# A hybrid decoder layer in three-product fp32: the mixer's values two heads at a time, and four smaller reorderings

## The chip, the cores and the metric

The kernel runs on one core of one Trainium2 chip. The metric is the time on the device in microseconds (us). Five engines work side by side, each through its own list of instructions: TensorE (PE; its weight loads are shown apart as PEld), VectorE (DVE), ScalarE (ACT), GpSimd (POOL) and SyncE (SP), which here issues most of the transfers.

## The reference

One layer of a decoder trunk for a prompt of 512 tokens and 8 samples of 8 tokens each (576 columns together, T; the prompt's 512 are TP, the samples' 64 are TS), model width 1024:

```python
# x -> x + post(Wout[concat(Mamba2-SSD heads, mLSTM heads)](pre(x)))   one combined input projection
# x -> x + post(CrossAttn(pre(x), memory K/V))
# x -> x + post(SwiGLU(pre(x)))                                        RMSNorm before and after each
SSM_HEADS, SSM_HEAD_DIM, SSM_GROUPS, SSM_STATE = 16, 64, 2, 128
ML_HEADS, ML_V_DIM, ML_QK_DIM = 4, 256, 128
N_MEM, X_HEADS, X_HEAD_DIM = 256, 4, 256
```

Three parts matter here. The SSD part computes for every head y = (C B^T * exp(segment sums, causal)) (dt x) plus the carried state's share. The mLSTM part has values v = u Wv of 4 heads x 256 columns. The cross attention of the prompt is softmax(q k^T) v over 256 memory rows, then a projection by the weights wxo.

## The kernel before, in words

Activations lie transposed in SBUF: 128 features by 576 columns, eight such blocks for the width. Every product of the projections is made of three matmuls: an operand is cast to a high part (`uh`, `whi`) and the rest is a low part (`ul`, `wlo`), and high x high, high x low and low x high are summed in PSUM. Weights come in units of 128 x 1024 (512 KB): `split_w` has SP load a unit into one of two buffers `raw`, ACT casts it to `whi` (L179), DVE takes the difference `wlo` (L186; in some tiles half of it is made by ACT and a transfer that adds). `whi` and `wlo` have three buffers each.

PSUM has eight banks of 512 columns: three in the pool `GP` (projections, values), three in `MP`, two in `BP`. A scheduler reorders the program by its own estimate of the times; `tc.issue_after(x)` makes what stands under it come later than x in that order, without a wait of its own. The order that it finds is fixed when the kernel is built; on the chip each engine takes its list in order and waits on semaphores.

The start (L295 to L346): `NWARM` dummy products warm PE up; the first two weight tiles come in quarters beside the blocks of x. Per block, ACT makes `uh` (L318) and DVE `ul` (L319); per quarter, a cast (L190) and a difference (L191). The products of these tiles are at L333 to L335. The fourth tile of the input weights, `w2`, is loaded whole into the buffer of the first (L336) and used at L200 to L203, the lines of the common `gemm`.

The values (`gemm_tok` with `v_evac`): for each of four heads two units of weights; the stationary operand is a block of tokens, the moving one the 256 columns of one head. Two token blocks share one bank. The 64 sample tokens use two narrower products instead of three. Each bank is copied out by ACT (L794), scaled by the norm.

The SSD part (`ssd_prompt`) runs over two groups and four pairs of heads. Per pair: `ps_l` (L615) spreads the segment sums, DVE adds the mask's terms (L618, four per head), ACT takes the exponential (L620), DVE multiplies by C B^T (L621), giving `lm`; then `ps_yi` (L626) is the product with x, `ps_ec` (L630) and `ps_yn` (L636) the carried state's share, which DVE multiplies (L638). The products of the values and, behind them, of the z projection (`ps_in`, L200 to L203) are put in between. What copies z out of its banks (L962 to L966) uses memory that the SSD part still holds, so those banks stay full until the last pair is done.

The attention: `ps_at` (scores, L1285 to L1287), their maximum and exponential `pr` (L1290 to L1294), `attn_values` with `ps_ov` (L1315 to L1317) and its split into `qh` and `ql` (L190, L191, into `oh`, `ol`). `ps_os` (L1342) are the samples' products with cached values, which come by transfers `kva` and `kvb`. `xo` (L1438) loads the weights wxo of the attention's output projection. `rstd_rows` (L243) spreads a norm's factors, one column per token block, over rows by transposes on PE (L251) and a copy.

## Time and profile before

| | |
|---|---|
| median of 3 runs | 1099.72 us (1099.5 to 1101.24) |
| the profiled execution | 1100.06 us |
| its span, first to last instruction | 1098.0 us |
| PE busy | 1087.5 us |
| PEld busy | 1041.8 us |
| DVE busy | 753.6 us |
| ACT busy | 610.3 us |
| POOL busy | 229.7 us |
| granted clock of PE | 0.998 |
| moved by the transfers | 181.25 MB |

The terms below are made against the profiled execution; 2.06 us of it lie outside its span. A row of a timeline has the start, the duration, the engine, the line, the operation with its tiles (output <- inputs), the shape, and how many alike follow each other (xN); in brackets, the idle time ahead of it on its engine and what ended it. Matmuls overlap, so the spacing of their starts, and not the duration, is what one costs. A row of waits has the sum, the number and the longest.

### The profile page before, as it was taken

The page shows a single profiled execution, that of the slowest core. Times are in us where ns is not written, and L with a number is a line of the kernel's source. Part 1 is how long each engine was busy: PE and PEld are TensorE (multiplying, and loading weights), DVE is VectorE, ACT ScalarE, POOL GpSimd, SP SyncE. Part 2 cuts the span into 40 slices and gives each one's busy share as a digit, 9 for nine tenths or more (in the row PEclk, how much of TensorE's full clock was granted, in tenths as well). Part 3 has the DMA queues.
Part 4 walks back from the last instruction along what each step waited for, and adds up shares of the span by engine and source line. Part 5 has one row for each costly group of instructions (what it writes and reads, how often), then busy time and mean ns, then how long its engine had stood idle before and what let it go on. Part 6 is the DMA issues. An engine that isn't in the chain of part 4 may idle for free.

```text
span 1098.0 us, 21177 instructions
## 1 busy us (share of the span) xinstructions
PE 1087.5 (99%) x8355; PEld 1041.8 (95%) x8355; DVE 753.6 (69%) x1507; ACT 610.3 (56%) x1105; POOL 229.7 (21%) x305
## 2 busy tenths in 40 slices
PE   9999999999999999999999999999999999999997
PEld 8999888998999999999988879999999999999997
DVE  6896776558877775659654456676557877788555
ACT  6877523346654565555544445645566566656654
POOL 1443544223213112000244301100011111111000
PEclk9999999999999999999999999999999999999999
DMA  6785544335745349553468764645386687578532
GB/s 211 186 148 128 154 144 155 125 88 154 203 137 162 102 146 310 183 194 102 153 206 282 252 223 156 227 165 114 93 199 139 144 199 180 120 181 191 130 130 87
DMA packets 58679, 181.25 MB, mean 165 GB/s; under 512 B 6572, under 2 KB 11820, under 8 KB 58068
## 3 DMA queue, kind: packets, MB, share of 16 engines
q1 hardware_dynamic: 42452, 136.85, 38.0%
q0 software_dynamic: 15552, 41.95, 19.4%
q8 instruction: 65, 1.06, 0.4%
q10 hardware_dynamic: 576, 1.11, 0.3%
q14 instruction: 34, 0.28, 0.1%
HBM read 159.23 MB, written 20.65 MB: 164 GB/s over the span
## 4 chain that ended last, share of the span: by engine, by line
PE 94%; DMA 3%; DVE 1%; ACT 1%; issue 0%; POOL 0%; SPq 0%; DVEq 0%; ACTq 0%; POOLq 0%
PE ps_in L200 7%; PE ps_in L201 7%; PE ps_in L203 7%; PE ps_o L201 3%; PE ps_o L203 3%; PE ps_o L200 3%; PE ps_g L1792 3%; PE ps_g L1793 3%; PE ps_g L1794 3%; PE ps_u L1792 3%; PE ps_u L1794 3%; PE ps_u L1793 3%; PE ps_dn L1792 2%; PE ps_dn L1793 2%; PE ps_dn L201 2%; PE ps_dn L200 2%
## 5 line engine op out<-in xcount | busy, mean ns | idle before, releaser
L200 PE MATMUL ps_in<-uh,whi 128*128 128x320 f32 (+1 forms) x544 | 163.6, 301 | 0.0
L203 PE MATMUL ps_in<-uh,wlo 128*128 128x320 f32 (+1 forms) x544 | 163.5, 301 | 0.0
L201 PE MATMUL ps_in<-ul,whi 128*128 128x320 f32 (+1 forms) x544 | 162.6, 299 | 0.0
L179 ACT CAST whi<-raw 128x1024 fp32r<-128x1024 f32 (+1 forms) x102 | 102.9, 1012 | 95.5 <-PE ps_in L201 28.6
L186 DVE TENSOR_TENSOR wlo<-raw,whi 128x512 fp32r<-128x512 f32 (+1 forms) x94 | 95.2, 1014 | 68.6 <-ACT whi L179 67.6
L200 PEld LDWEIGHTS ps_in<-uh,whi 128*128 128x128 f32 x544 | 103.1, 190 | 2.3 <-issue 1.7
L203 PEld LDWEIGHTS ps_in<-uh,wlo 128*128 128x128 f32 x544 | 103.1, 190 | 1.2 <-issue 0.4
L201 PEld LDWEIGHTS ps_in<-ul,whi 128*128 128x128 f32 x544 | 103.2, 190 | 0.6
L184 POOL DMA_DIRECT2D wlo<-win x32 | 27.7, 875 | 86.9 <-ACT wlo L183 78.8
L1792 PE MATMUL ps_g<-b,whi 128*128 128x288 f32 x144 | 42.5, 295 | 0.0
L1793 PE MATMUL ps_g<-b,whi 128*128 128x288 f32 x144 | 42.4, 295 | 0.0
L1793 PE MATMUL ps_u<-b,whi 128*128 128x288 f32 x144 | 42.4, 295 | 0.0
L1792 PE MATMUL ps_u<-b,whi 128*128 128x288 f32 x144 | 42.4, 295 | 0.0
L1765 ACT CAST whi<-rawx 128x1024 fp32r<-128x1024 f32 (+1 forms) x26 | 25.6, 986 | 27.8 <-PE ps_dn L1793 13.8
L191 DVE TENSOR_TENSOR wlo<-sw,whi 128x1024 fp32r<-128x1024 f32 (+1 forms) x26 | 29.6, 1139 | 14.9 <-ACT whi L190 14.8
L200 PE MATMUL ps_xo<-qh,whi 128*128 128x288 f32 x128 | 38.6, 303 | 0.2 <-ACT whi L179 0.2
L201 PE MATMUL ps_o<-mixs_l,whi 128*128 128x320 f32 (+1 forms) x128 | 38.2, 299 | 0.0
L203 PE MATMUL ps_o<-mixm_h,wlo 128*128 128x256 f32 (+1 forms) x128 | 38.2, 298 | 0.0
L201 PE MATMUL ps_xo<-ql,whi 128*128 128x288 f32 x128 | 37.9, 297 | 0.1
L201 PE MATMUL ps_xq<-u2l,whi 128*128 128x320 f32 (+1 forms) x128 | 38.0, 298 | 0.0
L201 PE MATMUL ps_o<-mixm_l,whi 128*128 128x256 f32 (+1 forms) x128 | 38.0, 296 | 0.0
L200 PE MATMUL ps_xq<-u2h,whi 128*128 128x320 f32 (+1 forms) x128 | 37.9, 300 | 0.0
(769 smaller groups left out, 3927.6 us busy)
## 6 DMA issues: line engine op xcount, KB each, us to landing
raw<-win SPq DMA_DIRECT2D x35, 512.0 KB, 3.7
raw<-wout SPq DMA_DIRECT2D x17, 512.0 KB, 3.6
raw<-wxq SPq DMA_DIRECT2D x13, 512.0 KB, 3.8
raw<-wgate SPq DMA_DIRECT2D x13, 512.0 KB, 4.4
raw<-wup SPq DMA_DIRECT2D x13, 512.0 KB, 5.1
wlo<-win POOLq DMA_DIRECT2D x24, 256.0 KB, 5.6
kva<-kc SPq DMA_DIRECT2D x12, 512.0 KB, 5.9
kva<-vc SPq DMA_DIRECT2D x12, 512.0 KB, 5.0
```

The lines of the kernel that those rows point to most:

```text
L179: A.copy(hi[:, :n], raw[:, :n])
L184: G.dma_start(lo[:, a:b], src[:, a:b], accum_op=ALU.add)
L186: e.tensor_tensor(lo[:, a:b], raw[:, a:b], hi[:, a:b].bitcast(F32), op=ALU.subtract)
L191: (eng or V).tensor_tensor(lo, src, hi.bitcast(F32), op=ALU.subtract)
L200: mm(ps, wh, ah, start=i == 0, stop=False)
L201: mm(ps, wh, al, start=False, stop=False)
L203: m = mm(ps, tiles[order[c]][1], xh(order[c], t0, n), start=False, stop=c == len(tiles) - 1)
L1765: A.copy(s.h3[:, s.all], s.r2[:, s.all])
L1792: mm(ps, wh, b[0][k], start=start and k == 0, stop=False, skip_group_check=True)
L1793: mm(ps, wh, b[1][k], start=False, stop=False, skip_group_check=True)
L1794: m = mm(ps, wl, b[0][k], start=False, stop=k == nk - 1, skip_group_check=True)
```

## The change

Five edits. (1) The start: 21 dummy products instead of 24; the first block of x is split in two halves; the quarters' casts and differences are put behind the copy of their block. (2) The values of two heads at once: the moving operand has 512 columns, one token block fills one bank; four units of weights per two heads; the first three token blocks go through units 0 to 3, then the last two through units 1, 2, 3 and 0, where unit 0 is loaded again. (3) Two calls of `rstd_rows` for the samples' norm spread only the samples' column. (4) `split` returns its cast. (5) The first three wxo weights are put behind the cast of the sixth attention output.

```diff
-NWARM = 24
+NWARM = 21
...
     def split(hi, lo, src, eng=None, cast=None):
-        (cast or A.copy)(hi, src)
+        c = (cast or A.copy)(hi, src)
         (eng or V).tensor_tensor(lo, src, hi.bitcast(F32), op=ALU.subtract)
+        return c
...
-        xd = (A if k < 2 else S).dma_start(xraw[:, k, :], I["xT"][:, k, :])
-        if k == 1:
+        xd = (S if k else A).dma_start(xraw[:, k, :], I["xT"][:, k, :])
+        if k % 2 == 0:
+            xd = (S if k else A).dma_start(raws[1][:, c], I["win"][2][:, c])
+        if k == 0:
...
+        for t0, n in ([(0, T)] if k else HALVES):
+            ts_ = slice(t0, t0 + n)
+            uhk = A.activation(uh[:, k, ts_], xraw[:, k, ts_], AF.Copy, scale=PAR("g_pre", k))
+            ulk = V.scalar_tensor_tensor(ul[:, k, ts_], xraw[:, k, ts_], PAR("g_pre", k), uh[:, k, ts_].bitcast(F32),
+                                         op0=ALU.mult, op1=ALU.subtract)
         if k % 2 == 0:
-            S.dma_start(raws[1][:, c], I["win"][2][:, c])
-            split(wi[0][0][:, c], wi[0][1][:, c], raws[0][:, c], cast=V.tensor_copy if k == 0 else None)
...
-        if k % 2 == 0:
-            split(wi[1][0][:, c], wi[1][1][:, c], raws[1][:, c])
+            for i in range(2):
+                with tc.issue_after(uhk.ins), tc.issue_after(ulk.ins):
+                    split(wi[i][0][:, c], wi[i][1][:, c], raws[i][:, c])
...
+        def products(u, c, first, last):
+            (hi, lo), (t0, n) = units[u], CHUNKS[c]
+            if first:
+                banks[c] = GP("ps_v")
+            ps = banks[c]
+            for i in range(2):
+                k, w = 2 * u + i, slice(512 * i, 512 * i + 512)
+                s_, e_ = first and i == 0, last and i == 1
                 if n == TS:
...
+                    mm(ps, U(k, t0, P), hi[:, w], start=s_, stop=e_, skip_group_check=True)
+                    mm(ps[:n], U(k, t0, n), lo[:, w], start=False, stop=e_, skip_group_check=True)
+                else:
+                    mm(ps, U(k, t0, n), hi[:, w], start=s_, stop=False, skip_group_check=True)
+                    mm(ps, UL(k, t0, n), hi[:, w], start=False, stop=False, skip_group_check=True)
+                    mm(ps, U(k, t0, n), lo[:, w], start=False, stop=e_, skip_group_check=True)
...
+        for u in range(4):
+            with tc.issue_after(added[0].ins) if g == 0 and u < 2 else ExitStack():
+                unit(u)
+            for c in range(3):
+                products(u, c, u == 0, u == 3)
+        for u in (1, 2, 3, 0):
+            for c in (3, 4):
+                products(u, c, u == 1, u == 0)
+            if u == 1:
+                unit(0)
+
+    for g in range(2):
+        values(g)
...
-            split(oh[:, j, 0:TP], ol[:, j, 0:TP], pso)
+            ovs.append(split(oh[:, j, 0:TP], ol[:, j, 0:TP], pso))
...
-        rstd_rows(rc2[1], HCHUNKS[1], rb2, B1)
+        rstd_rows(rc2[1][:, 2:3], HCHUNKS[1][2:], rb2, B1)
...
-    m = xq(7, 1)
-    with tc.issue_after(m.ins):
-        rstd_rows(rc2[0], HCHUNKS[0], rb2, B1)
+    xq(7, 1)
...
-        with tc.issue_after(evx[j - 3].ins) if j > 2 else ExitStack():
+        with tc.issue_after(evx[j - 3].ins if j > 2 else ovs[5].ins):
```

The lists of the engines move with it. In the changed file the lines of the common functions are one higher (L200 is L201), later ones about 5, and from the values on about 29 higher. ACT at the start, before; `uh` are the copies of the blocks, `whi` the casts of the quarters:

```order
L318 ACTIVATE uh<-xraw,par 128x576 x2
L190 CAST whi<-raw 128x256 x2
L318 ACTIVATE uh<-xraw,par 128x576
L190 CAST whi<-raw 128x256
L318 ACTIVATE uh<-xraw,par 128x576
L190 CAST whi<-raw 128x256
L318 ACTIVATE uh<-xraw,par 128x576
L190 CAST whi<-raw 128x256
```

ACT at the same place, after:

```order
L321 ACTIVATE uh<-xraw,par 128x256
L321 ACTIVATE uh<-xraw,par 128x320
L190 CAST whi<-raw 128x256 x2
L321 ACTIVATE uh<-xraw,par 128x576 x2
L190 CAST whi<-raw 128x256 x2
L321 ACTIVATE uh<-xraw,par 128x576 x2
L190 CAST whi<-raw 128x256 x2
L321 ACTIVATE uh<-xraw,par 128x576 x2
L190 CAST whi<-raw 128x256 x2
```

Blocks and casts go in twos, and the first cast, which DVE made before, is ACT's. PE around the masks of the last pair of heads in the SSD part, before:

```order
L201 MATMUL ps_in<-ul,whi 128x320
L615 LDWEIGHTS c_81
L615 MATMUL ps_l<-cumst,c_81 128x512
L203 MATMUL ps_in<-uh,wlo 128x320
L615 LDWEIGHTS c_81
L615 MATMUL ps_l<-cumst,c_81 128x512
L200 MATMUL ps_in<-uh,whi 128x320
```

From that last row on, 42 products of `ps_in` follow before `ps_yi` of the pair. PE there, after, from the pair before to the last one:

```order
L631 MATMUL ps_yi<-lm,xdt 64x128 x8
L635 LDWEIGHTS c_81
L635 MATMUL ps_ec<-cumst,c_81 64x384
L635 LDWEIGHTS c_81
L635 MATMUL ps_ec<-cumst,c_81 64x384
L641 MATMUL ps_yn<-bc,hs 128x128 x3
L620 LDWEIGHTS c_81
L620 MATMUL ps_l<-cumst,c_81 128x512
L620 LDWEIGHTS c_81
L620 MATMUL ps_l<-cumst,c_81 128x512
L631 MATMUL ps_yi<-lm,xdt 64x128 x8
```

No `ps_in` is left in between. One pair earlier, 3 products of 320 and 24 of 256 columns stand between `ps_l` and `ps_yi`, and ACT has the cast of a z weight ahead of the first exponential of that pair. ACT in the attention, between the probabilities of one head and the scores of the next, before:

```order
L190 CAST prh<-ps_pt 128x512
L179 CAST whi<-raw 128x1024
L190 CAST qh<-ps_ov 128x512 x2
L179 CAST whi<-raw 128x1024
L1294 ACTIVATE pr,sm<-ps_at,mx,scol 128x256 x2
```

ACT there, after:

```order
L190 CAST prh<-ps_pt 128x512
L190 CAST qh<-ps_ov 128x512 x2
L179 CAST whi<-raw 128x1024 x2
L1324 ACTIVATE pr,sm<-ps_at,mx,scol 128x256 x2
```

The cast of the wxo unit that stood ahead of the copies of `ps_ov` stands behind them.

More of the change, by code (lines that the diff above doesn't have):

```diff
@@ L309, in build @@
             S.dma_start(raws[0][:, c], I["win"][1][:, c])
-        xd = (A if k < 2 else S).dma_start(xraw[:, k, :], I["xT"][:, k, :])
-        if k == 1:
+        xd = (S if k else A).dma_start(xraw[:, k, :], I["xT"][:, k, :])
+        if k % 2 == 0:
+            xd = (S if k else A).dma_start(raws[1][:, c], I["win"][2][:, c])
+        if k == 0:
             with tc.issue_after(xd.ins), tc.high_priority(offset=300):
                 A.activation(sp.tile([P, 1], F32, name="one"), wz[:, 0:1], AF.Exp)
-        if k % 2 == 0:
-            S.dma_start(raws[1][:, c], I["win"][2][:, c])
-            split(wi[0][0][:, c], wi[0][1][:, c], raws[0][:, c], cast=V.tensor_copy if k == 0 else None)
-        uhk = A.activation(uh[:, k, 0:T], xraw[:, k, :], AF.Copy, scale=PAR("g_pre", k))
-        ulk = V.scalar_tensor_tensor(ul[:, k, :], xraw[:, k, :], PAR("g_pre", k), uh[:, k, 0:T].bitcast(F32),
-                                     op0=ALU.mult, op1=ALU.subtract)
-        if k % 2 == 0:
-            split(wi[1][0][:, c], wi[1][1][:, c], raws[1][:, c])
+        for t0, n in ([(0, T)] if k else HALVES):
[3 more added lines that the diff above has]
+                                         op0=ALU.mult, op1=ALU.subtract)
+        if k % 2 == 0:
+            for i in range(2):
+                with tc.issue_after(uhk.ins), tc.issue_after(ulk.ins):
+                    split(wi[i][0][:, c], wi[i][1][:, c], raws[i][:, c])
     S.dma_start(c32, I["c32"][:, 0:NLONG])
@@ L767, in gemm_tok @@
         units = units or [split_w(src[:, i, :], cut=cut) for i in range(2)]
-        for c0 in range(0, len(chunks), 2):
-            ps = GP("ps_v")
-            for c, (t0, n) in enumerate(chunks[c0:c0 + 2]):
-                if n == TS:
-                    for k in range(KT):
-                        hi, lo = units[k // 4]
-                        j = (k % 4) * 256
-                        mm(ps[:, 0:256], xh_(k, t0, P), hi[:, j:j + 256], start=k == 0, stop=k == KT - 1, skip_group_check=True)
-                        mm(ps[:n, 0:256], xh_(k, t0, n), lo[:, j:j + 256], start=False, stop=k == KT - 1, skip_group_check=True)
-                    break
-                for k in range(KT):
-                    hi, lo = units[k // 4]
-                    j = (k % 4) * 256
-                    ah, al = xh_(k, t0, n), xl_(k, t0, n)
-                    o = ps[:n, c * 256:c * 256 + 256]
-                    mm(o, ah, hi[:, j:j + 256], start=k == 0, stop=False, skip_group_check=True)
-                    mm(o, al, hi[:, j:j + 256], start=False, stop=False, skip_group_check=True)
-                    m = mm(o, ah, lo[:, j:j + 256], start=False, stop=k == KT - 1, skip_group_check=True)
-            evac(c0, ps)
@@ L788, in gemm_tok @@
-        return m
-    def v_evac(h):
-        def ev(c, ps):
-            if c < 4:
-                for i in range(2):
-                    A.activation(vt4[:, c + i, h, 0:256], ps[:, 256 * i:256 * i + 256], AF.Copy, scale=rx[:, c + i:c + i + 1])
-            else:
-                A.copy(vts[:TS, h, 0:256], ps[TS:P, 0:256])
-                V.tensor_tensor(vts[:TS, h, 0:256], vts[:TS, h, 0:256], ps[:TS, 0:256], op=ALU.add)
-                A.activation(vts[:TS, h, 0:256], vts[:TS, h, 0:256], AF.Copy, scale=rx[:TS, 4:5])
-        return ev
@@ L801, in build @@
-    for h in range(4):
-        with tc.issue_after(added[0].ins) if h == 0 else ExitStack():
-            units = [split_w(I["wv"][h][:, i, :], cut=1024) for i in range(2)]
-        gemm_tok(I["wv"][h], U, UL, CHUNKS, v_evac(h), units=units)
+        ps = GP("ps_v")
+        for c, (t0, n) in enumerate(chunks):
+            for k in range(KT):
+                hi, lo = units[k // 4]
+                j = (k % 4) * 256
+                ah, al = xh_(k, t0, n), xl_(k, t0, n)
+                o = ps[:n, c * 256:c * 256 + 256]
+                mm(o, ah, hi[:, j:j + 256], start=k == 0, stop=False, skip_group_check=True)
+                mm(o, al, hi[:, j:j + 256], start=False, stop=False, skip_group_check=True)
+                m = mm(o, ah, lo[:, j:j + 256], start=False, stop=k == KT - 1, skip_group_check=True)
@@ new lines, in gemm_tok, with values, unit @@
+        evac(0, ps)
+        return m
+    def values(g):
+        units, banks = {}, {}
+        def unit(u):
+            units[u] = split_w(I["wv"][g][:, u, :], cut=1024)
+        def products(u, c, first, last):
[6 more added lines that the diff above has]
+                s_, e_ = first and i == 0, last and i == 1
+                if n == TS:
+                    mm(ps, U(k, t0, P), hi[:, w], start=s_, stop=e_, skip_group_check=True)
[4 more added lines that the diff above has]
+                    mm(ps, U(k, t0, n), lo[:, w], start=False, stop=e_, skip_group_check=True)
+            if not last:
+                return
+            p2 = ps.rearrange("p (h k) -> p h k", h=2)
+            if n == TS:
+                o = vts[:TS, 2 * g:2 * g + 2, 0:256]
+                A.copy(o, p2[TS:P])
+                V.tensor_tensor(o, o, p2[:TS], op=ALU.add)
+                A.activation(o, o, AF.Copy, scale=rx[:TS, 4:5])
+            else:
+                A.activation(vt4[:, c, 2 * g:2 * g + 2, 0:256], p2, AF.Copy, scale=rx[:, c:c + 1])
+        for u in range(4):
[8 more added lines that the diff above has]
+                unit(0)
@@ L1265, in build @@
     oh, ol = qh, ql
+    ovs = []
     scol = at.tile([P, 4], F32, name="scol")
@@ L2197, in _quarters, with _halves @@
     return np.ascontiguousarray(w.reshape(2, 4, P, 4, 256).transpose(3, 2, 0, 1, 4).reshape(4, P, 2, 1024))
+def _halves(w):
+    return np.ascontiguousarray(w.reshape(4, 2, P, 2, 512).transpose(3, 2, 0, 1, 4).reshape(2, P, 4, 1024))
 def _feat(x):
@@ L2236, in pack @@
     out["win"] = _units(np.concatenate([gate, xbc[:, 1024:], xbc[:, :1024], q, k, z, og], 1), KT)
-    out["wv"] = _quarters(v)
+    out["wv"] = _halves(v)
     out["wmk"] = _units(i["w_mem_k"][0], KT)
```

## The prediction

> **What bounds the kernel now.** I read the head of the page first, then its chain, then what TensorE (PE) waited for, then the timelines of single places. Head of the page and the shares of the chain:

> ```profile
> span 1098.0 us, 21177 instructions
> PE 1087.5 (99%) x8355; PEld 1041.8 (95%) x8355; DVE 753.6 (69%) x1507; ACT 610.3 (56%) x1105; POOL 229.7 (21%) x305
> PE 94%; DMA 3%; DVE 1%; ACT 1%; issue 0%; POOL 0%; SPq 0%; DVEq 0%; ACTq 0%; POOLq 0%
> ```

> PE is busy in 99% of the span, and the chain runs through it for 94%. All waits of PE that the trace names:

> ```profile
> PE ps_at L1285 <- DVE ql L191: 1.6, 1, 1.6
> PE ps_warm L301 <- DVE wz L298: 1.1, 1, 1.1
> PE ps_os L1342 <- DMA kva<-vc: 0.3, 1, 0.3
> PE ps_xo L200 <- ACT whi L179: 0.2, 1, 0.2
> ```

> They are 3.2 us in all. So a change can gain only what it takes off PE's own work and at most these waits; and whatever makes PE stand anywhere is paid in full, since PE has no slack later to make it up. VectorE (DVE) and ScalarE (ACT) have slack on average, but not in every chain of steps. I therefore go through the five edits by what PE does beside them.

> **The start.** Timeline of the first 20 us (start, duration, engine, line, operation):

> ```profile
> 1.06 5.09 PE L301 MATMUL ps_warm<-wz 128*128 128x256 bf16 x24 [1.06 <-DVE wz L298]
> 5.91 0.51 PE L333 MATMUL ps_in<-uh,whi 128*128 128x256 f32 x2
> 11.66 0.39 ACT L190 CAST whi<-raw 128x256 fp32r<-128x256 f32 x1
> 12.06 0.78 ACT L318 ACTIVATE uh<-xraw,par 128x576 fp32r<-128x576 f32 x1
> 12.74 0.39 ACT L190 CAST whi<-raw 128x256 fp32r<-128x256 f32 x1
> 12.53 0.42 DVE L191 TENSOR_TENSOR wlo<-raw,whi 128x256 fp32r<-128x256 f32 x1
> 12.97 7.21 SPq L174 DMA_DIRECT2D raw<-win x3
> 17.52 1.05 ACT L179 CAST whi<-raw 128x1024 fp32r<-128x1024 f32 x1 [0.60 <-DMA raw<-win]
> 19.54 0.31 PE L201 MATMUL ps_in<-ul,whi 128*128 128x320 f32 x1
> 19.88 0.38 PE L203 MATMUL ps_in<-uh,wlo 128*128 128x256 f32 x1
> ```

> Before, the 24 warming products run until the first real product at 5.91. Three fewer take off 3 x 0.21 us (5.09 / 24), and halves of the first block of x come sooner: the first product can start at about 5.55. I give that gain no value, since PE is caught again at 19.88. There it waits for the low half of the fourth weight tile (0.34 us behind the product before it, where 0.15 is the usual spacing of this form: 0.2 us lost). That tile's transfer can be issued only when the raw buffer is free, and that is when the low half of the last quarter of the first tile is formed: DVE 12.53 to 12.95, SP issues at 12.97, ACT casts at 17.52 directly after the landing. In the changed order two more items stand on ACT ahead of that quarter's cast: one more cast (0.40 us, 11.66 to 12.06) and one more copy (0.68 us, 12.06 to 12.74). So the cast moves from 11.66 to about 12.75, the issue from 12.97 to about 14.1, and PE's 19.88 to between 20.4 (a shorter landing: the transfer is queued behind less) and 21.0. **+0.6**, between -0.4 (the tile is not waited for, the start is the gain) and +1.2.

> **The values.** Before, 128 x 3 products at lines 784 to 786 and 32 x 2 at 776 and 777, 256 columns each: 448. Groups by form, and the timelines that show the spacing; the two rows of L1315 and L1317 are the first and last of nine 512-column products of the attention in a row:

> ```profile
> L784 PE MATMUL ps_v<-whi,uh x128: 278/283/472, 166.3 to 238.3; 128*128 128x256 f32 x128
> L776 PE MATMUL ps_v<-whi,uh x32: 277/278/364, 184.2 to 240.3; 128*128 128x256 f32 x32
> 235.68 0.28 PE L786 MATMUL ps_v<-wlo,uh 128*128 128x256 f32 x1
> 238.67 0.28 PE L776 MATMUL ps_v<-whi,uh 128*128 128x256 f32 x1
> 624.12 0.63 PE L1315 MATMUL ps_ov<-prh,mv 128*128 128x512 f32 x2
> 625.97 0.39 PE L1317 MATMUL ps_ov<-prh,mv 128*128 128x512 f32 x1
> 626.19 0.28 PE L1285 MATMUL ps_at<-mk,qh 128*128 128x256 f32 x1
> ```

> The duration of a product (0.28) overlaps the next; what counts is the spacing. From 235.68 to 238.67 there are 25 products: 2.99 / 25 = 0.120 us. From 624.12 to 626.19 nine wide ones: 2.07 / 9 = 0.230 us. Before: 448 x 0.120 = 53.6 (the 64 narrow ones run at 0.117, which takes 0.2 off: 53.4). After: 224 x 0.230 = 51.5. **-1.9**, with single spacings of 0.226 to 0.232 us between -1.4 and -2.8. The two further loads (ten units instead of eight: one cast of 1.05 us on ACT and one difference on DVE each) lie beside PE work in a stage where the three-deep buffers hold a unit ahead; if that cover went, it is a wait, and is priced as a rival. [...]

> **The last head pairs of the Mamba part.** Here the loss comes in. Two pairs, in two views of the timeline (PE first, then DVE):

> ```profile
> 235.12 0.61 PE L615 MATMUL ps_l<-cumst,c 80*128 80x512 bf16 x2
> 241.82 1.09 PE L626 MATMUL ps_yi<-lm,xdt 128*64 128x128 f32 x16
> 243.01 0.94 PE L636 MATMUL ps_yn<-bc,hs 128*128 128x128 f32 x6
> 243.70 0.36 PE L201 MATMUL ps_in<-ul,whi 128*128 128x256 f32 x1
> 235.54 2.16 DVE L618 SCALAR_TENSOR_TENSOR lm<-ps_l,ncum,c 128x128 f32<-128x128 f32 x8 [1.76 <-PE ps_l L615]
> 237.62 1.47 DVE L621 TENSOR_TENSOR lm<-lm,cbs 128x512 f32<-128x512 f32 x2
> 244.08 0.56 DVE L638 TENSOR_TENSOR ec<-ec,ps_yn 128x384 f32<-128x384 f32 x1 [0.37 <-ACT ec L633]
> ```

> A pair's ps_yi needs both masks lm; these take 235.12 to 239.09, 4.0 us after ps_l. In the kernel before, more than 40 products of the z projection stand between ps_l and ps_yi of the last pair, and PE never waits. In the changed order the last pair's two ps_l are followed at once by its ps_yi: the values are already finished, and the three banks of the pool that z uses are full until after the last pair. PE's work from the ps_yi of the pair before to that point is 243.70 - 241.82 = 1.88 us and two ps_l (0.47). DVE stands behind L638 of the pair before, which ends 2.82 us after that ps_yi began (244.64 - 241.82); then eight L618 (237.62 - 235.54 = 2.08) and two L621 (1.47): 6.4 us. PE stands 6.4 - 2.35 = 4.0 us; at least 3.5, if DVE could begin as soon as ps_l is there. [...] Together **+4.7**, between +3.5 and +5.4. The products of z that fill these holes before are still to be done behind them.

> **The norm's rows.** Timeline:

> ```profile
> 536.83 0.58 PE L251 MATMUL ps_rb<-c,p_r 128*128 128x128 f32 x3
> 537.33 0.38 PE L201 MATMUL ps_xq<-u2l,whi 128*128 128x256 f32 x1
> ```

> Three transposes take 0.50 us of PE's row; two of them go, and two others at 545 us: 4 x about 0.1. **-0.4**, between -0.2 and -0.6. The copies on ACT that also shrink lie off the path.

> **The casts tied behind the copy of attention outputs.** Timeline of SP, PE, ACT and DVE there:

> ```profile
> 619.81 0.33 SPq L174 DMA_DIRECT2D raw<-wxo x1
> 630.20 0.63 PE L1342 MATMUL ps_os<-kva 128*32 128x256 f32 x6
> 632.45 0.39 PE L1285 MATMUL ps_at<-mk,qh 128*128 128x256 f32 x1 [1.62 <-DVE ql L191]
> 629.49 1.05 ACT L179 CAST whi<-raw 128x1024 fp32r<-128x1024 f32 x1 [7.09 <-DMA raw<-wxo]
> 630.44 1.07 ACT L190 CAST qh<-ps_ov 128x512 fp32r<-128x512 f32 x2
> 631.71 1.28 DVE L191 TENSOR_TENSOR ql<-ps_ov,qh 128x512 fp32r<-128x512 f32 x2
> ```

> ps_ov was finished at about 626.2 (the ps_at at 626.19 follow it), but its copy to qh had to stand on ACT behind the cast of a wxo weight that waited 7.09 us for its transfer (issued at 619.81 behind four loads of kva and kvb); ql was late, and PE stood 1.62. The tie puts the copy first: qh at about 627.4, ql at about 628.3, ahead of the second ps_at on PE. On SP, the loads of kva behind the held wxo transfers also go out earlier, so the 0.3 at ps_os should go. **-1.9**, between -2.4 and 0. What is next late is the exponential of the scores behind two tied casts (2 x 1.05 us).

> **The sum.** +0.6 - 1.9 + 4.7 - 0.4 - 1.9 = +1.1 on the profiled execution of 1100.06: 1101.2. It lies 0.34 above the median of 1099.72, so against the median I forecast 1100.8. About 0.2% (2.2 us: 1097.5 and 1101.9) is what a measurement of this kernel can tell from no change; the forecast is no change.

> **Rivals.**

> A, the stand at the last pairs does not show. For it: DVE is busy in only 69% of the span, so that its chain may run ahead of what my rows add up; and what DVE, ACT and the transfers do while PE stands may spare PE small pauses in the next stage. Against it: the chain is of rows with nothing between them, and PE keeps its order. Then 1100.8 - 4.7 = 1096.1, faster. Chance 0.25.

> B, slower: on ACT, a cast of a z weight now stands ahead of the exponential of the mask of the last pair but one, and another ahead of the one before. ACT takes its instructions in order (see the cast at 629.49 that held the copy), so a transfer that lands late holds lm and PE with it. Loads of this kind land in the median after:

> ```profile
> raw<-win SPq DMA_DIRECT2D x35, 512.0 KB, 3.7
> ```

> The load is issued shortly before ps_yi of the preceding pair, and the cast is wanted some 4.5 us later (1.88 and 18 products of 0.147): it decides from a landing of over 5 us on, with the cast of 1.05 behind it. The fourth tile of the start took about 4.5 (12.97 to 17.5), the wxo load nearly ten (619.81 to 629.49). Halfway, some 3 us more: 1103.8. Chance 0.15.

> C, the clock. The three warming products fewer and a hole of 0.3 us ahead of the first product could postpone the full clock, which the trace shows by the spacing of the products soon behind 5.91. The warming products run at 0.21 us for 256 columns, later ones at 0.120. If the slow rate went on for as long again as from the first warming product to the first real one less the hole, some 4 us, about 4 x (1 - 0.120 / 0.21) = 1.7 us of work would be lost, of which the wait at the fourth tile (0.2 before, 0.6 more now) hides 0.8: 1100.8 + 0.9 = 1101.7. Chance 0.05. [...]

> D, the tie does nothing for PE: the two casts behind the copy, or a transfer behind them, delay the exponential of the next scores by what was saved. For it, the cast at 629.49 shows wxo transfers as late as that; against it, PE has two products' groups of other heads ahead of them. 1100.8 + 1.9 = 1102.7. Chance 0.09.

> E, the wide products do not pay: their spacing in this stage is near twice the narrow one (0.237 us, where the attention's rows gave at most 0.232), so that 224 of them take 53.1 us and the gain is 0.3. 1100.8 + 1.6 = 1102.4. Chance 0.03, since both spacings are measured at neighbouring products of the same kind. [...]

> **How the numbers follow.** The forecast has 0.43, with its own terms from 1098.5 to 1102.3. Faster by over 0.2%: A and a little of the forecast's low end, 0.28. Within: most of the forecast and C, 0.40. Slower: B, D, E and the forecast's upper end, 0.32. The range for 8 in 10 reaches from A (with the values at their better end, 1095.6) to above D (1103.2) and leaves out most of B and the edge of A.

> **What would show it.** PE's waits should name ps_yi behind DVE lm with 3.5 to 4 us once and 0.2 to 1.4 once; ps_in of the fourth tile behind DVE wlo with 0.6 to 1.5 near 20 us; ps_at behind ql should be gone. Wide ps_v products should be spaced 0.226 to 0.232. If no ps_yi wait is there, A holds; if ps_yi waits 5 us or more and the cast ahead of the exponential ends late, B; if the first products are spaced at twice 0.120 behind 5.5 us, C. If PE waits for a values' weight, the supply that I took as covered was the error.

## The result, and the profile after

The change makes the kernel slower by 0.3%: 1102.89 us (median of 14 runs, 1101.44 to 1105.46) against 1099.99 us (14 runs, 1098.75 to 1101.24); the ratio is 1.003, with an interval of 1.0022 to 1.0038. The forecast was 1100.8 and no change. The time lies inside the range that was given, but the change is slower, clear of the noise. The profiled execution took 1103.3 us and has a span of 1101.5 us.

PE has fewer products than before (8124 after 8355) and loses more to waits than it saves. Head of the page of the changed kernel, and what PE waited for (sum, number, longest):

```profile
span 1101.5 us, 20717 instructions
PE 1086.5 (99%) x8124; PEld 1029.5 (93%) x8124; DVE 753.0 (68%) x1507; ACT 610.9 (55%) x1096; POOL 229.9 (21%) x305
```

```profile
PE ps_yi L631 <- DVE lm L626: 4.8, 2, 3.8
PE ps_in L201 <- ACT whi L179: 0.6, 1, 0.6
PE ps_in L204 <- DVE wlo L186: 0.5, 1, 0.5
```

The wait for ql and that for kva are gone from the list. New are the two holes at the last pairs of heads, 4.8 us together, and two waits for the fourth weight tile at the start. The holes in PE's timeline, and what DVE did in the larger one:

```profile
249.49 1.09 PE L631 MATMUL ps_yi<-lm,xdt 128*64 128x128 f32 x16 [1.01 <-DVE lm L626]
251.45 0.60 PE L620 MATMUL ps_l<-cumst,c 80*128 80x512 bf16 x2
255.88 1.98 PE L631 MATMUL ps_yi<-lm,xdt 128*64 128x128 f32 x16 [3.83 <-DVE lm L626]
258.11 1.65 PE L641 MATMUL ps_yn<-bc,hs 128*128 128x128 f32 x6
252.20 2.15 DVE L623 SCALAR_TENSOR_TENSOR lm<-ps_l,ncum,c 128x128 f32<-128x128 f32 x8
254.27 1.47 DVE L626 TENSOR_TENSOR lm<-lm,cbs 128x512 f32<-128x512 f32 x2
```

From ps_yi of the pair before (249.49) to that of the last (255.88) it takes 6.39 us. But look at the durations: the same sixteen ps_yi took 1.09 us ahead of the hole and 1.98 behind it. The windows of the changed kernel show why (length, busy time of PE, PEld, DVE, ACT, POOL, then the granted clock of PE):

```profile
250.00:254.00 4.00, 2.05 (x22) 1.29 (x17) 3.02 (x9) 1.12 (x2) 0.98 (x1) 1.00 0.94 278
254.00:260.00 6.00, 4.12 (x26) 3.50 (x27) 2.52 (x6) 1.32 (x3) 0.18 (x2) 0.50 0.70 284
260.00:262.00 2.00, 2.00 (x15) 2.00 (x14) 2.00 (x5) 1.98 (x5) 1.50 (x3) 0.79 0.00 0
```

The clock fell to half inside the hole, at 254.0, and came back at 260.8 (a mean of 0.79 over two us is half speed for 0.84 of them). For 5 us PE worked behind the hole at half its rate.

Where the time went, by stage, from the starts of PE's products (us from one first product to the next):

| stage, ended by the first | before | after | change without wide values | wide values alone | tied casts and norm rows alone |
|---|---|---|---|---|---|
| ps_h (start, projections) | 108.37 | 109.02 | 109.64 | 109.33 | 109.44 |
| ps_o (values, SSD, mLSTM) | 281.87 | 288.23 | 282.05 | 288.82 | 281.87 |
| ps_sa (output projection, norm) | 155.01 | 154.99 | 154.59 | 155.43 | 154.59 |
| ps_os (samples' scores) | 68.27 | 67.94 | 68.59 | 68.77 | 68.89 |
| ps_g (attention, wxo) | 85.84 | 82.36 | 82.36 | 84.67 | 82.32 |
| the rest | 390.63 | 390.62 | 390.63 | 390.62 | 390.63 |

One stage loses 6.4 us, one wins 3.5. The first row counts from the first dummy product. The profile of the wide values alone is the slowest of its five executions (1107.78 us; their median is 1105.27).

### The profile page after: what moved, and what is told of

Same layout as the page of the kernel before. It is cut to its first block, busy times and chain, and to the rows that moved or that the text cites. A ratio compares the mean times of both kernels' runs of the same rounds, so it can differ in the third digit from the quotient of the medians.

```text
span 1101.5 us, 20717 instructions
## 1 busy us (share of the span) xinstructions
PE 1086.5 (99%) x8124; PEld 1029.5 (93%) x8124; DVE 753.0 (68%) x1507; ACT 610.9 (55%) x1096; POOL 229.9 (21%) x305
## 3 DMA queue, kind: packets, MB, share of 16 engines
q8 instruction: 64, 1.05, 0.4%
## 4 chain that ended last, share of the span: by engine, by line
PE 95%; DVE 2%; DMA 1%; ACT 1%; issue 0%; SPq 0%; DVEq 0%; ACTq 0%
PE ps_in L201 6%; PE ps_in L202 6%; PE ps_in L204 6%; PE ps_o L202 3%; PE ps_g L1820 3%; PE ps_g L1822 3%; PE ps_g L1821 3%; PE ps_o L204 3%; PE ps_o L201 3%; PE ps_u L1820 3%; PE ps_u L1822 3%; PE ps_u L1821 3%; PE ps_dn L1820 2%; PE ps_dn L1821 2%; PE ps_dn L202 2%; PE ps_dn L201 2%
## 5 line engine op out<-in xcount | busy, mean ns | idle before, releaser
L179 ACT CAST whi<-raw 128x1024 fp32r<-128x1024 f32 (+1 forms) x104 | 105.2, 1013 | 119.0 <-PE ps_in L202 39.3
L201 PE MATMUL ps_in<-uh,whi 128*128 128x320 f32 (+1 forms) x544 | 163.8, 301 | 0.6 <-ACT whi L179 0.6
L201 PEld LDWEIGHTS ps_in<-uh,whi 128*128 128x128 f32 x544 | 103.2, 190 | 3.9 <-issue 2.1
L191 DVE TENSOR_TENSOR wlo<-sw,whi 128x1024 fp32r<-128x1024 f32 (+1 forms) x26 | 29.6, 1140 | 15.0 <-ACT whi L190 14.9
L201 PE MATMUL ps_xo<-qh,whi 128*128 128x288 f32 x128 | 38.5, 302 | 0.2 <-ACT whi L179 0.2
L201 PE MATMUL ps_o<-mixs_h,whi 128*128 128x320 f32 (+1 forms) x128 | 37.8, 295 | 0.2 <-DVE tmp L1034 0.2
L201 PE MATMUL ps_xq<-u2h,whi 128*128 128x320 f32 (+1 forms) x128 | 37.9, 300 | 0.0
L201 PE MATMUL ps_o<-mixm_h,whi 128*128 128x256 f32 (+1 forms) x128 | 37.9, 296 | 0.0
## 6 DMA issues: line engine op xcount, KB each, us to landing
raw<-win SPq DMA_DIRECT2D x35, 512.0 KB, 3.6
raw<-wout SPq DMA_DIRECT2D x17, 512.0 KB, 3.6
raw<-wxq SPq DMA_DIRECT2D x13, 512.0 KB, 4.1
raw<-wgate SPq DMA_DIRECT2D x13, 512.0 KB, 3.7
raw<-wup SPq DMA_DIRECT2D x13, 512.0 KB, 5.0
kva<-kc SPq DMA_DIRECT2D x12, 512.0 KB, 5.8
kva<-vc SPq DMA_DIRECT2D x12, 512.0 KB, 6.9
```

The source lines that it names most:

```text
L179: A.copy(hi[:, :n], raw[:, :n])
L191: (eng or V).tensor_tensor(lo, src, hi.bitcast(F32), op=ALU.subtract)
L201: mm(ps, wh, ah, start=i == 0, stop=False)
```

## The experiments

Theory O: the order left PE without products at the last two pairs, and the hole took the clock with it. Against it stood S (the wide values cost by themselves), M (the loss sits in the order of the mLSTM stage) and I (the lower clock is of no account). "Before" ran beside every kernel; its medians were 1100.4 to 1100.8, and 1099.99 beside the changed kernel. Kernels are therefore compared by their distance from the "before" beside them; for the change it is +2.9 us.

**Without the wide values**, and **the wide values alone.** The edits are the parts of the diff as shown above.

> The change without the wide values: new start, norm rows, tied casts. Theory O: +0.6 at the start, -0.4 norm, -3.5 attention: about 1096.7, and no ps_yi wait. Rival M: the mLSTM part is slower here too, 1099 or more.

Measured: 1097.93 us, ratio 0.9975 (0.9964 to 0.9986), 2.5 us under before, though 1.2 above what O gave. PE has no ps_yi wait; the stage up to ps_o takes 282.05 us.

> The kernel before with the wide values alone. Theory O: products -2.4, holes +5, clock +2.5, some 0.5 of disorder in the next stage: about 1105.5, with ps_yi waits of about 4.8 us. Rival M: 1101 to 1103, the holes partly made up. Rival S: slower too, but with PE waiting for whi or wlo of the values, not for lm.

Measured: 1105.27 us, ratio 1.0042 (1.0028 to 1.0055), 4.9 us above before. The longest waits of PE but for the one ahead of the dummy products:

```profile
PE ps_yi L626 <- DVE lm L621: 4.8, 2, 3.8
PE ps_ov L1339 <- ACT prh L190: 0.9, 2, 0.7
```

The loss of that stage comes with the wide values and with the wait for lm, and no wait names a weight of the values. M and S as expected are out; but it isn't shown yet that the hole, and not its company, is what costs.

**Another order for the same work.**

```diff
+            with tc.issue_after(masks[{0: 13}[u]].ins) if g == 1 and u in {0: 13} else ExitStack():
+                for c in (3, 4):
+                    products(u, c, u == 1, u == 0)
...
+        with tc.issue_after(masks[{1: 15}[j]].ins) if j in {1: 15} else ExitStack():
+            in_tile(21 + j, z_evac(j))
```

(`masks` collects the ps_l products; 13 and 15 are the last of the last two pairs. The first condition holds for the last ten wide products, the second for the second z tile.)

> The changed kernel with the last ten wide products of the values ordered behind the masks (ps_l) of the last pair but one, and the second z tile behind the masks of the last pair, so that PE has products in both holes. Theory O (the order left PE without work, and the clock fell behind the 3.8 us hole): the waits of ps_yi shrink from 4.8 to about 1.1 us, the clock stays at full speed, 1102.9 - 3.7 - 2.5 = about 1096.7. Rival S (the wide products or the two further weight units cost more than they save, whatever the order): 1102 to 1103. Rival M (the loss sits later, in the mLSTM part's order): about 1100.5, the clock part stays.

Measured: 1098.19 us, ratio 0.998 (0.9971 to 0.9989): 2.2 us under before, where the change is 2.9 above it, with the same products. Waits of PE:

```profile
PE ps_in L204 <- DVE wlo L186: 1.3, 2, 0.8
PE ps_yi L632 <- DVE lm L627: 1.2, 1, 1.2
PE ps_in L201 <- ACT whi L179: 1.2, 1, 1.2
...
PE ps_in L204 <- DMA wlo<-win: 0.4, 1, 0.4
```

O holds: one hole of 1.2 us is left, for the 1.1 that was expected, and the clock stayed (0.999 over the run). It is 1.5 us short of the forecast. The wait for whi and 0.5 of that for wlo lie at the start; between 234 and 245 us PE now waits 0.8 and 0.4 for the low half of z's weights, which z uses earlier, and 0.3 for a bank: new waits for part of the old.

**The clock by itself.** Dummy products in the hole, ahead of ps_yi on PE:

```diff
+            if g == 1 and j == 3:
+                for _ in range(12):
+                    with tc.issue_after(masks[-1].ins):
+                        mm(psi, sel[:80, 0:1].to_broadcast([80, P]), cumst[:, 0:TP], start=True, stop=True,
...
```

(They write the bank that ps_yi then overwrites. ps_ec of that pair is tied behind its ps_yi, where it stood before.)

> The changed kernel with twelve dummy products (80 rows, 512 columns, bf16, about 2.6 us together) behind the last pair's masks, in the hole of PE. The hole's end is set by VectorE and does not move. Theory O: PE's clock stays full because the idle rest is only some 1.2 us; the products behind run at full rate: 1102.9 - 2.5 = about 1100.4. Rival I (the idle time alone costs, the lower clock in the trace is of no account): 1102.9, no change.

Measured: 1099.99 us, ratio 0.9994 (0.9985 to 1.0003): 0.4 us under before, where the change is 2.9 above it, by work that computes nothing. Its windows:

```profile
254.00:256.00 2.00, 1.29 (x8) 0.41 (x6) 1.83 (x5) 0.81 (x2) 0.00 (x0) 1.00 1.04 424
256.00:258.00 2.00, 2.00 (x25) 1.73 (x26) 0.75 (x1) 0.49 (x1) 0.00 (x0) 1.00 0.99 409
```

Theory I falls. But with twelve the scheduler also ordered the next stage otherwise. With nine or fewer, and with eight and four, PE's list is the changed kernel's but for the dummies.

> The changed kernel with only four dummy products (about 0.9 us) behind the last masks, so that PE's idle rest is about 2.9 us instead of 3.8. If the clock falls only behind an idle stretch longer than that: full clock, about 1100.4, as with twelve. If 2.9 us are enough for it: 1102.5 to 1103.

Measured: 1103.48 us, ratio 1.0022 (1.0012 to 1.0032), 2.7 us above before: as the change. The wait left at the last pair is 2.4 us, and the clock fell all the same:

```profile
256.00:258.00 2.00, 1.23 (x12) 1.23 (x14) 0.69 (x1) 0.00 (x0) 0.00 (x0) 0.50 1.01 413
```

> The changed kernel with eight dummy products (about 1.8 us) behind the last masks; unlike with twelve, every other product of PE stands in the very order of the changed kernel. PE's idle rest is about 2 us. If the clock holds: the clock's part of the loss alone goes, about 2.4 us: 1100.5, and what is still different in the next stage with that order (0.5 to 1) stays. If the clock falls as with four: 1103.

Measured: 1103.58 us, ratio 1.004 (1.0023 to 1.0058), 3.1 us above before; three of the ten executions lie at 1107.33 to 1111.3. The wait left is 1.6 us, and the clock fell with it, at 256.56 (0.64 over the two us from 256).

> The changed kernel's order with nine dummy products in the hole before the last pair: an idle rest of about 1.4 us there, 1.2 us in the hole before. If a little less idle time than with eight is enough for the clock to hold: about 1100.5; else 1103.5 as with eight.

> The changed kernel's order with eight dummy products in the hole before the last pair and four among the products before the pair ahead of it, so that that smaller hole shrinks from 1.2 to about 0.3 us; the rest of PE's list is as in the changed kernel. If the clock goes by PE's activity summed over a stretch of some us, which takes in both holes, it holds now: 1102.9 - 2.4 = about 1100.5. If it goes by the last hole alone (1.6 us, as with eight alone, where it fell): 1103.5.

Measured: 1101.63 us, ratio 1.0012 (1.0004 to 1.0021), with nine; 1102.46 us, ratio 1.0018 (1.0008 to 1.0029), with eight and four. Neither answer of the expectations holds for every execution. With eight and four, four executions lie at 1100.39 to 1100.63 and eight at 1102.11 to 1105.34; the profiled one is of the first kind, with a full clock. The mean granted clock of the four is 0.997 or 0.998, that of the eight 0.995 to 0.997. With nine the times spread from 1100.25 to 1103.79; its profile, too, has a full clock. In the profiles of the change and of the kernel before the clock changes on a grid of 3.41 us that does not begin with the hole (the last section has the times). Below is the step of that length, on the grid of its own profile, that holds most of the wait, with its length and PE's busy time ahead of the other engines', in the profiles of the change, of four and of eight dummies:

```profile
250.60:254.01 3.41, 1.45 (x10) 0.86 (x8) 3.03 (x10) 1.12 (x2) 0.98 (x1) 1.00 1.01 310
252.24:255.66 3.42, 1.81 (x10) 0.67 (x8) 3.07 (x11) 1.01 (x3) 0.99 (x1) 1.00 1.03 312
253.14:256.56 3.42, 1.85 (x10) 0.64 (x9) 3.26 (x10) 1.26 (x2) 0.98 (x1) 1.00 1.04 380
```

With nine, with twelve, and with eight and four:

```profile
251.78:255.19 3.41, 2.44 (x11) 0.84 (x9) 3.30 (x11) 1.26 (x2) 0.98 (x1) 1.00 1.06 336
252.47:255.88 3.41, 2.75 (x12) 1.07 (x11) 3.31 (x11) 1.26 (x2) 0.98 (x1) 1.00 1.03 367
253.45:256.87 3.42, 1.85 (x22) 1.10 (x20) 2.13 (x6) 0.99 (x2) 0.00 (x0) 1.00 1.03 420
```

Behind each of the first three the clock fell (to 0.50, 0.50 and 0.64 over the two us from 254, 256 and 256), behind none of the others (1.00). With nine the end of a step, at 255.19, cuts the wait of 1.4 us in two; with eight the wait of 1.6 lies in one step whole. That the hole lies otherwise in the grid from one execution to the next would explain that, near this amount, one kernel gives both kinds; only one execution of each was profiled, so this is not shown. But 1.85 us stand on both sides (with ten products in the step that brought the fall, 22 in the other), so busy time alone does not decide; what does stays open.

The stage up to ps_o takes 285.77 us with nine and 288.23 in the change, with the same order of products: 2.5 us is the price of the fallen clock (half rate over the 5 us of work behind the hole gives as much). With twelve dummies the stage takes 284.59 us: another 1.2 us lie in the next products' order (ps_nh + 1.1, ps_in + 0.7, ps_cu - 0.7 and smaller ones), which twelve dummies and the other order above did not have.

**The tied casts and the norm rows alone.**

> The kernel before with the tied casts and the shorter norm rows alone. If the traces are read rightly, -3.5 and -0.4: about 1096.3, the wait of ps_at for ql gone. The prediction's own terms, -1.9 and -0.4, would give 1097.9.

Measured: 1096.8 us, ratio 0.9966 (0.9954 to 0.9979), 4.0 us under before and the fastest of all. The first expectation holds. The two edits were not run apart.

**The start alone.**

> The kernel before with the new start alone. The traces so far lose 0.6 to 1.3 us up to the end of the fourth tile: 1100.8 to 1101.5. If the earlier first product counted, 1099.8.

Measured: 1101.63 us, ratio 1.0008 (0.9997 to 1.0019). That leans to the slower side and is not settled. The profiles don't settle it either: the product that waits for the low half of the fourth tile, with the new start alone (first) and with the old start in the kernel of the tied casts (second):

```profile
19.83 0.38 PE L203 MATMUL ps_in<-uh,wlo 128*128 128x256 f32 x1 [0.21 <-DVE wlo L186]
```

```profile
20.94 0.38 PE L204 MATMUL ps_in<-uh,wlo 128*128 128x256 f32 x1 [0.46 <-DVE wlo L186]
```

The spread from one execution to another, a microsecond, is as large as the effect. Over all profiles, the stage up to ps_h takes 108.35 to 109.44 us with the old start (five, mean 108.8) and 108.33 to 109.99 with the new one (nine, mean 109.3). The kernel without the wide values differs from the one with tied casts and norm rows by the new start alone, and gains less (2.5 against 4.0 us, with intervals that overlap). All of this leans to some tenths lost.

**Can the wide values pay?** Two more orders, both with the old start and with the products of z split by hand: the first tile's 256 columns ahead of the masks of the last pair but one (or behind them), 15 and then 9 of its 320-column products behind the masks of the last two pairs. The second z tile is held back as above.

```diff
+    for (t0, n), ka, at_ in zip(HALVES, (8, 5), (13, 15)):
+        ps = GP("ps_in")[:, :n]
+        if ka:
+            gemm(ps, [(*w, KT)], U, UL, t0, n, 0, ka)
+        with tc.issue_after(masks[at_].ins):
+            if ka < KT:
+                gemm(ps, [(*w, KT)], U, UL, t0, n, ka, KT)
+        ev(t0, n, ps)
```

> All parts of the change but the new start, with the products of z spread by hand: the first z tile and its weights' first use behind the masks of the last pair but one, its last nine products and the next tile behind the masks of the last pair. Every hole then has 4 to 5 us of products. Theory O: no ps_yi wait over 0.3 us, full clock, values -2.4, norm -0.4, attention -3.5: about 1094 (against 1100.2 before). Rival S (the wide values cost elsewhere): no better than the kernel with tied casts and norm rows alone, 1096 or more, with PE waiting for weights of the values or of z.

(Here `(0, 5)` stands for `(8, 5)`, and the values are not held back.) Measured: 1100.59 us, ratio 0.9997 (0.9988 to 1.0006), far off. The profiled execution is the slowest of its eleven (1102.47 us, the fastest took 1098.14); what follows explains that one. Its longest wait of PE, and ACT there:

```profile
PE ps_l L617 <- ACT ec L635: 3.0, 1, 3.0
```

```profile
240.54 1.04 ACT L179 CAST whi<-raw 128x1024 fp32r<-128x1024 f32 x1 [2.52 <-DMA raw<-win]
242.23 0.49 ACT L635 ACTIVATE ec<-ps_ec 128x384 f32<-128x384 f32 x1
```

A cast on ACT waited 2.52 us for a z weight; the exponential of ps_ec stood behind it, and ps_l behind that for its bank. This is the mechanism of the prediction's rival B, in another kernel; the clock fell behind the hole here too (0.79 from 240 to 245).

> All but the new start, wide values; the last ten wide products of the values, and 15 of z, behind the masks of the last pair but one, nine of z and the next tile's 24 behind the masks of the last pair. Holes have 4.2 to 4.5 us of products. If z's weights come in time: ps_yi waits under 0.3 us, full clock: 1096.8 (tied casts and norm rows alone) - 2.4 = about 1094.5. If z's weights are late for the earlier use, as in the first such order (1.5 us of waits for wlo): 1096 to 1097, and the wide values bring nothing.

(Here the last ten wide products are held back as above.) Measured: 1098.0 us, ratio 0.9979 (0.997 to 0.9988). Waits of PE:

```profile
PE ps_yi L628 <- DVE lm L623: 0.9, 2, 0.5
PE ps_in L204 <- DVE wlo L186: 0.8, 1, 0.8
PE ps_in L335 <- DVE ul L320: 0.6, 1, 0.6
PE ps_in L204 <- DMA wlo<-win: 0.5, 1, 0.5
PE ps_in L201 <- ACT vt L816: 0.3, 1, 0.3
```

The second expectation holds in its direction; the time is 1.0 us beyond its range. Up to ps_o it takes 283.07 us, where the narrow values take 281.87. The values save 1.8 here (spacings of ps_v: 53.53 after 55.32), and the waits of this stage take back 2.5: 1.3 for z's weights, 0.3 for a bank, 0.9 for the masks (the 0.6 for ul lies at the start). Another 0.5 is not named. That z's weights come later because two more units of values are loaded ahead of them is argued, not tried. Of what was run, the best kernel is the one before with the tied casts and the shorter norm rows: 1096.8 us, better than both.

## Why the prediction was wrong

**The bound.** That PE has no slack, so that a hole is paid in full, was right. That a hole costs its own length and no more was the error.

**The start, +0.6.** In the profiled execution every link came as worked out:

```profile
13.95 6.87 SPq L174 DMA_DIRECT2D raw<-win  x3
18.16 1.05 ACT L179 CAST whi<-raw 128x1024 fp32r<-128x1024 f32 x1 [1.49 <-DMA raw<-win]
20.51 0.38 PE L204 MATMUL ps_in<-uh,wlo 128*128 128x256 f32 x1 [0.46 <-DVE wlo L186]
```

The issue moved from 12.97 to 13.95, PE's product from 19.88 to 20.51: +0.63. With the old start and the tied casts the product stood at 20.94, so the profile of before was an early one. How far the term holds for the mean of executions stays open, as said.

**The values, -1.9.** Sixteen spacings of the wide products:

```profile
180.06 0.39 PE L809 MATMUL ps_v<-wlo,uh 128*128 128x512 f32 x1
183.69 0.39 PE L807 MATMUL ps_v<-whi,uh 128*128 128x512 f32 x1
```

3.63 / 16 = 0.227 us, at the better end of what the attention's products had shown. All spacings of ps_v in the stage sum to 52.92 us after 55.32: -2.4. For comparison, the dummy products of the runs with nine and with eight and four, bf16 with 512 columns, start 0.215 to 0.216 us apart.

**The last head pairs, +4.7.** Waits of 3.83 and 1.01 us, 4.8 together, for 4.0 and 0.7. No run shows the 0.7 that +4.7 has for the last pair but one; the change showed the 1.01 us there. (Products of 320 columns do start 0.147 us apart in the profile of before, as rival B has it: 0.44 us for three, from 18.71 to 19.15.) For the last pair the step was right, to its reasons: from one ps_yi to the next it is 6.39 us, for 6.4. **The step that failed is the one behind it:** what follows a hole was taken to run at its usual rate. I held the clock to be a matter of the start alone (rival C), although the profile gave the slower rate (0.21 us for 256 columns at the warming products, where the trace has the full clock from 5.82 us on), and the hole was forecast as 4 us long. The missing term is +2.5 us, from the profiles with nine dummies and with none. The trace shows the fall in the hole of 3.83 us; the runs with four and eight dummies show it with waits of 2.4 and 1.6 us at that place, too.

**The next stages, 0.** What the stage up to ps_o lost beyond the terms above, 6.4 + 2.4 - 4.8 - 2.5 = +1.5, was not forecast at all; 1.2 of it is the other order behind the last pair. Nor were +0.4 in the output projection (ps_o, 102.62 to 103.02) and -0.3 up to ps_os.

**The norm, -0.4.** Of the two calls of `rstd_rows` one now spreads only the samples' column and the other is gone, as the diff behind it shows: 8 transposes instead of 12. ps_rb in that stage went from 1.42 to 0.98.

**The attention, -1.9.** The direction and place were right, the size was not: -3.5 in the profiles (85.84 to 82.36). ACT and PE there after:

```profile
631.52 1.07 ACT L190 CAST qh<-ps_ov 128x512 fp32r<-128x512 f32 x2 [4.25 <-PE ps_ov L1347]
632.48 1.06 ACT L179 CAST whi<-raw 128x1024 fp32r<-128x1024 f32 x1
635.21 0.28 PE L1315 MATMUL ps_at<-mk,qh 128*128 128x256 f32 x1
```

I counted only waits that the list of waits named, 1.9 us. Of the 3.5 us, 2.4 are in the spacings of ps_os, the named 1.6 among them (one spacing of 2.00, where others of that kind take 0.31), and 0.9 in those of ps_xo, with the named 0.3. The other 1.6 are parts of spacings that the list doesn't name, as 0.07 us of that one (2.00, less the wait of 1.62 and 0.31); what the others come from is not shown. Spacings summed by tile would have shown them.

**The sum by its terms**: +0.6 - 2.4 + 4.8 + 2.5 + 1.5 + 0.4 - 0.3 - 0.4 - 3.5 = +3.2. In the profiles the last product of PE starts 3.2 us later; the medians differ by 2.9. That the time came within 2.1 us of the forecast is luck in part: the clock and the order were missed by 4.0 us, and the attention and the values by 2.1 the other way. Of the rivals, A fell with the two waits. B's late transfer did not hold the masks in the changed kernel itself. C was about the clock, as 2.5 us of the loss were, but at the wrong place: at the start the trace has the full clock from 4.84 us on, where it was 5.82 in the kernel before. D and E were off: the casts paid, and the wide products came at the good end of their term.

## What to carry to other kernels

Where an engine is busy for 99%, its list of products is a stock of cover for the chains of other engines: shorter products use it up sooner, and the place to look is the last chain behind which no cover is left. A hole of some microseconds on TensorE is to be priced with the half-rate stretch behind it as well (here 2.5 us behind a hole of 3.83). Enough cheap products in the hole (twelve here; four and eight were too few), or better some real ones held back, save that price. And a queue that takes its work in order should not have a cast that waits for a transfer ahead of what TensorE waits for: tying such casts behind the copy was nearly the whole gain of the best kernel here (3.5 of 4.0 us).

## What the runs showed of the hardware

The half rate lasted one or two such steps: 6.83 us in the change, where PE was busy for 1.54 us of the first of them, and 6.8 us with four dummies (by the shares of 0.91, 0.50, 0.50, 0.50 and 0.88 in the windows of 2 us from 254 on); 3.4 us with eight dummies (0.64 and 0.51 in the two windows from 256 on) and in the first of the two late orders (0.79 and 0.87 over the 5 us from 240 and from 245), where PE was busy from the fall on. Which steps at full clock bring the fall, the profiles bound but do not settle. In the change the one with PE busy for 1.45 us did, and those with 2.32 (18.50 to 21.91, at the fourth weight tile) and 2.41 us (247.18 to 250.60, with the smaller hole) did not. In the kernel before, one with 1.79 (630.46 to 633.87, around the wait of 1.62 us in the attention) did not. With the steps shown above, there is a fall behind 1.45, 1.81 and 1.85 us, and none behind 1.79, 1.85, 2.32 and more.
